# One packed copy in a decoder-layer kernel, issued one tile later behind an order edge

## The chip, the cores and the metric

The kernel runs on one core of a Trainium2 chip. The metric is the device time of one execution in microseconds (us). Three executions before the change took 2226.68, 2227.14 and 2234.79 us, so the median is 2227.14 us. One more execution was taken with the hardware profiler.

## The reference

The reference is one decoder layer on x of 4096 rows by 1024, in float32:

```python
h = _rms(x, norm_gain[l]); proj = h @ w_in[l]          # 1024 -> 3328 columns
y_g = _chunked_gmlp(g_u, g_v, ...) * silu(g_gate)       # 4 heads x 64, chunks of 128 rows
q = _rms(a_q, attn_q_gain); k = _rms(a_k, attn_k_gain)  # 8 heads x 64
y_a = _dilated_attention(q, k, v) * silu(a_gate)        # (window, dilation) = (128,1), (512,4), (2048,16)
y_m = _memory_attention(m_q, mem, ...) * silu(m_gate)   # 4 heads, 256 memory tokens
x = x + concat(y_g, y_a, y_m) @ w_out[l]
```

Queries and keys are normalised for each head (root mean square over 64 values), and the dilated attention reads them in three strides: every row, every 4th and every 16th.

## The kernel before

The 4096 rows are cut into 32 tiles of 128 rows (`NT`). Every large projection is done with 16-bit operands, a value being split into a high and a low part, so that one tile against 512 columns is 24 matmuls (`proj`, L219 to L223).

The work is traced in stages. Pass A (L384 to L459) goes over the 32 tiles: it normalises and transposes three tiles ahead (`rows`), projects the values (`pv`, stored to `vd`), and projects queries and keys of heads 0 to 3 (`pq`). Pass B (`pass_b`) does the queries and keys of heads 4 to 7 (`pqb`) and the attention gates (`pag`). Pass C does the two other branches, and a last loop the output projection (`fps`). The attention proper (`attn_all`) is a generator whose steps are traced between those of pass B and pass C (`merge`) with a higher priority. In it `attn_max` (L465) finds row maxima, and `attn_main` (L533) computes scores, exponentials (`e`, L580), their high part (`ph`, L529) and low part (`pl`, L530) and the products with the values.

The change touches `qk_out` (L292), which both passes call once for each tile, 64 times in all. For a tile n:

- `head_rs` copies the projection out of PSUM on ScalarE (`rw_q`, L257), squares it (L259), sums on VectorE (L261), and takes a power on GpSimd (L269); VectorE multiplies (L276, L278).
- ScalarE casts the result to 16 bit (`hl`, L296), VectorE subtracts for the low part (L297).
- SyncE issues a DMA transpose of `hl` into one half of `stg` (L299). A `stg` tile holds a pair of tiles; there are two of them.
- ScalarE copies this half of `stg` into `stp` with its columns in another order (L300). This is the packed copy. There is one `stp`.
- After the second tile of a pair SyncE issues three stores: `knd` and `qnd` from `stg` (L304, L305) and `qkpd` from `stp` (L306).

In pass A each eighth tile also issues `load_max` for head 0 (L317), which loads back what eight tiles have stored. `attn_max` and `attn_main` of later heads load from the same DRAM tensors.

Each engine runs its instructions in one order, and all DMAs are issued from SyncE's queue, also in one order. That order is not the traced one: a scheduler goes over the whole program with a simulated timeline and takes, for each engine, what is ready by its own times, by priority; the priority is the place in the trace, moved ahead by 400 for the attention steps. Dependences between tiles are found by the framework. An order edge without synchronisation (`tc.issue_after(ins)`) tells the scheduler that what is traced in its block on the engine of `ins` stands behind `ins`.

Of the kernel before, what the change touches and what calls it, by code (L numbers as in the profile page):

```python
# [18 lines left out]
P = 128  # L19
T = 4096  # L20
D = 1024
NT = T // P
# [18 lines left out]
R16 = 16  # L41
# [30 lines left out]
def tile_hybrid_layer(ctx, tc, x, mem, norm_gain, w_in, gv_gain, wsT, gb, aqg, akg,  # L72
                      mem_gain, w_kv, mqg, mkg, w_out, out):
    nc = tc.nc
    V, S, G, TE, Q = nc.vector, nc.scalar, nc.gpsimd, nc.tensor, nc.sync
# [6 lines left out]
    def ps_tile(tag, shape, dt, name):  # L82
        return pp.tile(shape, dt, tag="po" if tag == "tr" else tag, name=name)
# [3 lines left out]
    kn_d = [dp.tile([4, P, T], F16, name=f"knd{g}") for g in range(2)]  # L87
    qn_d = [dp.tile([4, 64, T], F16, name=f"qnd{g}") for g in range(2)]
    qkp_d = [dp.tile([8, P, T], F16, name=f"qkpd{g}") for g in range(2)]
# [109 lines left out]
    def start_job(key, tag, cols, gain, gaina, src=None, pt="pj", pool=None, gap=0):  # L199
        box = []  # L200

        def mk():
            if not box:
                box.append(wtile(tag, 256 * len(cols), key))
            return box[0]

        jobs.append(prep_job(key, [(mk, 256 * i, w_in if src is None else src, c, gain, gaina)
                                   for i, c in enumerate(cols)], pt, pool, gap))
        next(jobs[-1])

    def tick():
        for j in list(jobs):
            if next(j, 1) == 1:
                jobs.remove(j)

    def got(key):
        return ready[key][0][0], [sc for _, sc in ready[key]]

    def proj(ps, xt, w, n, c=0):  # L219
        for k in range(KT):  # L220
            for a, b in ((0, 0), (0, 1), (1, 0)):
                TE.matmul(ps[:, :n], xt[:, a, k, :], w[:, b, k, c:c + n],  # L222
                          start=(k == 0 and a == 0 and b == 0), stop=(k == KT - 1 and a == 1))  # L223
# [50 lines left out]
    def qk_split(pool, ps, nh, scs, nm, gain=None, glo=0):  # L274
        r, qn = head_rs(pool, ps, nh, scs, [S24] * len(scs), nm)
        V.tensor_tensor(qn, qn, bcast(r, HD), ALU.mult)  # L276
        if gain is not None:
            V.tensor_mul(qn[:, glo:nh, :], qn[:, glo:nh, :], gain)  # L278
        return qn
# [9 lines left out]
    sk = ctx.enter_context(tc.tile_pool(name="sk", bufs=2))  # L289
    pm = ctx.enter_context(tc.tile_pool(name="pm", bufs=2))  # L290

    def qk_out(pool, ps, n, g, scs, stgs):  # L292
        stg, stp = stgs
        qn = qk_split(pool, ps, 8, scs, f"q{g}_{n}", agn, 4)
        hl = pool.tile([P, 8, 2, HD], F16, name=f"hl{g}_{n}", tag="hl", bufs=2)
        S.copy(hl[:, :, 0, :], qn)  # L296
        V.tensor_sub(hl[:, :, 1, :], qn, hl[:, :, 0, :])  # L297
        half = slice((n % 2) * P, (n % 2 + 1) * P)
        Q.dma_start_transpose(stg[:, :, half], hl.rearrange("p s a c -> p (s a c)"))  # L299
        S.copy(stp[:, :, half].rearrange("p s (r j) -> p s r j", r=R16),  # L300
               stg[:, :, half].rearrange("p s (j r) -> p s r j", r=R16))
        if n % 2 == 1:
            cc = slice((n - 1) * P, (n + 1) * P)
            Q.dma_start(kn_d[g][:, :, cc].rearrange("s p t -> p s t"), stg[:, 4:8, :])  # L304
            Q.dma_start(qn_d[g][:, :, cc].rearrange("s p t -> p s t"), stg[0:64, 0:4, :])  # L305
            Q.dma_start(qkp_d[g][:, :, cc].rearrange("s p t -> p s t"), stp)  # L306

    def stages(n):
        return (pm.tile([P, 8, 256], F16, name=f"stg{n}", tag="stg", bufs=2),
                pm.tile([P, 8, 256], F16, name=f"stp{n}", tag="stp", bufs=1))  # L310
# [6 lines left out]
    def load_max(h, c0, c1):  # L317
        g, s = h // 4, h % 4
        if h not in heads:
            heads[h] = (sk.tile([P, T], F16, name=f"qn_{h}", tag="qn", bufs=1),  # L320
                        sk.tile([P, T], F16, name=f"kp_{h}", tag="kp", bufs=1))
        qn, kp = heads[h]
        Q.dma_start(kp[:, c0:c1], qkp_d[g][4 + s, :, c0:c1])
        Q.dma_start(qn[0:64, c0:c1], qn_d[g][s, :, c0:c1])
        Q.dma_start(qn[64:128, c0:c1], qn_d[g][s, :, c0:c1])
# [11 lines left out]
    with tc.tile_pool(name="pA", bufs=2) as pA:  # L337
# [44 lines left out]
        stg = None  # L382
        mTs = sk.tile([P, 2, 2, KT, P], F16, name="mTs", tag="q1", bufs=1)
        for n in range(NT):  # L384
# [45 lines left out]
            if n % 2 == 0:  # L430
                stg = stages(f"A{n}")
            qk_out(pm, ps, n, 0, scQ0, stg)
            if n % 8 == 7:
                load_max(0, (n - 7) * P, (n + 1) * P)
            tick()
            if n == 5:
# [4 lines left out]
            if n == 12:  # L441
                wM, scM = got("wM")
                for j in range(2):
# [5 lines left out]
                    hl = pm.tile([P, 8, 2, HD], F16, name=f"mhl{j}", tag="hl", bufs=2)  # L449
# [228 lines left out]
    def pass_b():  # L678
        xTs = {}
        wQ1, scQ1 = got("wQ1")  # L680
        stg = None
        for n in range(NT + LAG):
            if n < NT:
                xT = sk.tile([P, 2, KT, P], F16, name=f"xTb{n}", tag="xT", bufs=4)
                Q.dma_start(xT.rearrange("p a k t -> p (a k t)"), xT_d[n])
                xTs[n] = xT
                ps = ps_tile("pj", [P, 512], F32, f"pqb{n}")
                proj(ps, xT, wQ1, 512)
                if n % 2 == 0:
                    stg = stages(f"B{n}")  # L690
                qk_out(pm, ps, n, 1, scQ1, stg)
                yield
            tick()
            if n == 2:
                wAG, scAG = got("wAG")
                for i in range(2):
                    V.tensor_scalar_mul(hsc[:, i:i + 1], scAG[i][:, 2:3], 0.5)
                    V.tensor_mul(fag[:, i:i + 1], hsc[:, i:i + 1], scV[i][:, 0:1])
                    V.tensor_scalar_mul(fag[:, i:i + 1], fag[:, i:i + 1], 2.0 ** -4)
            if n >= LAG:  # L700
                m = n - LAG
                ps = ps_tile("pj", [P, 512], F32, f"pag{m}")
                proj(ps, xTs.pop(m), wAG, 512)
                sg = pm.tile([P, 512], F32, name=f"sg{m}", tag="sg", bufs=2)
                for i in range(2):
                    S.activation(sg[:, i * 256:(i + 1) * 256], ps[:, i * 256:(i + 1) * 256],
                                 AF.Tanh, scale=hsc[:, i:i + 1])
                V.scalar_tensor_tensor(sg, sg, 1.0, ps, ALU.add, ALU.mult)
                Q.dma_start(ag_d[m], sg)
                yield  # L710
            if n == 6:
                start_job("wC1", "w1", (C_GV, C_MQ), ng, nga)
            if n == 16:
                start_job("wC3", "wc", (C_MG,), ng, nga)
            if n == NT - 1 + CS:
                start_job("wC2", "w2", (C_GU, C_GG), ng, nga, gap=1)

    merge(tc, pass_b(), side, 190/62.0, 2)

    yTs = {}  # L720
# [270 lines left out]
```

## Time and profile before

| | |
|---|---|
| median of three executions | 2227.14 us |
| profiled execution | 2231.72 us, of which its span is 2230.0 us |
| mean granted TensorE clock | 0.966 of full speed |
| TensorE matmul busy | 2031.2 us (91%) |
| VectorE busy | 1459.8 us (65%) |
| ScalarE busy | 1200.2 us (54%) |
| GpSimd busy | 684.2 us (31%) |
| DMA traffic | 341 MB, mean 153 GB/s |

The profiled execution lies 4.6 us above the median and between the fastest and the slowest of the three. In the trace, PE is TensorE's matmul part, PEld its weight load, DVE VectorE, ACT ScalarE, POOL GpSimd and SP SyncE; "q" behind an engine's name is its sequencer. L300 is line 300 of the kernel. Busy matmul time is modelled at its ends, so idle PE time is the surer reading.

### The profile page before, as it was taken

To read this page: it belongs to the slowest core of one execution; us is meant where nothing else is said; L and a number is where in the kernel's file an instruction comes from. 1 tells how busy PE (TensorE), PEld (TensorE's weight loads), DVE (VectorE), ACT (ScalarE), POOL (GpSimd) and SP (SyncE) were. 2 spreads that over 40 slices of the span, in tenths; PEclk is the share of its full clock that TensorE was granted. 3 is DMA by queue.
4 is the path that set the end of the run, shared out by engine and by line. 5 is a ranking of instruction groups with operands and counts; after the bars stand their busy time and mean duration, and the time that the engine had idled before them with its cause. 6 is when DMAs were issued, how large, how long until landed. Compare 5 with 4: busy or idle time off the path is not lost. (4 is left out here: it accounts for less than half of the span.)

```text
span 2230.0 us, 45732 instructions
## 1 busy us (share of the span) xinstructions
PE 2031.2 (91%) x17025; PEld 1297.4 (58%) x17025; DVE 1459.8 (65%) x4331; ACT 1200.2 (54%) x2048; POOL 684.2 (31%) x632
## 2 busy tenths in 40 slices
PE   5989989889889898899999898998997999999999
PEld 4435444334346455465676675775764766666676
DVE  7555564365657676477786677875876667777662
ACT  6666565343457577476565565664655763222221
POOL 1212212121035355253454453553543551000000
PEclk8999999999899999999999999999998999999999
DMA  7767676484565865755646447536435337777662
GB/s 228 198 152 207 167 187 163 115 212 121 153 145 136 205 147 130 202 119 146 167 98 138 116 94 169 114 94 151 97 90 124 89 97 219 222 218 220 205 187 75
DMA packets 468959, 341.00 MB, mean 153 GB/s; under 512 B 294400, under 2 KB 404096, under 8 KB 466944
## 3 DMA queue, kind: packets, MB, share of 16 engines
q1 hardware_dynamic: 468736, 338.08, 58.8%
q8 instruction: 133, 2.18, 0.4%
q14 instruction: 90, 0.74, 0.1%
HBM read 198.52 MB, written 113.84 MB: 140 GB/s over the span
## 5 line engine op out<-in xcount | busy, mean ns | idle before, releaser
L530 POOL TENSOR_TENSOR pl<-e,ph 128x512 f16<-128x512 f32 (+1 forms) x384 | 413.1, 1088 | 359.2 <-ACT ph L529 265.2
L222 PE MATMUL pc<-wC,xTc 128*128 128x512 f16 (+1 forms) x2304 | 473.3, 349 | 6.3 <-DVE zm L899 5.2
L483 DVE CUSTOM_DVE_ANT_0 jk<-pa,mask 128x256 bf16<-128x256 f32 (+1 forms) x768 | 299.8, 390 | 86.1 <-PE pa L476 66.2
L222 PE MATMUL fps<-wO,fyT 128*128 128x256 f16 (+1 forms) x2304 | 341.0, 309 | 0.3 <-DVE fa L746 0.3
L222 PEld LDWEIGHTS <-xTc 128*128 128x128 f16 x2304 | 221.5, 100 | 161.6 <-issue 16.8
L580 ACT ACTIVATE e<-e,gas 128x512 f32<-128x512 f32 (+1 forms) x384 | 254.0, 674 | 112.5 <-DVE e L578 110.5
L578 DVE TENSOR_TENSOR e<-s,mask 128x512 f32<-128x512 f32 (+1 forms) x384 | 234.1, 626 | 77.8 <-PE s L575 68.3
L222 PEld LDWEIGHTS <-fyT 128*128 128x128 f16 x2304 | 224.5, 98 | 103.3 <-issue 1.7
L222 PEld LDWEIGHTS <-xTa 128*128 128x128 f16 x1608 | 159.4, 100 | 205.8 <-issue 42.3
L222 PEld LDWEIGHTS <-xTb 128*128 128x128 f16 x1536 | 150.8, 100 | 174.3 <-issue 29.1
L269 POOL TENSOR_TENSOR r_q<-r_q,mhalf 128x8 f32<-128x8 f32 x64 | 113.2, 1769 | 422.5 <-DVE r_q L267 406.9
L529 ACT CAST ph<-e 128x512 f16<-128x512 f32 (+1 forms) x384 | 211.9, 568 | 18.0 <-PE o L600 11.7
L222 PE MATMUL pqb<-wQ,xTb 128*128 128x512 f16 x768 | 191.6, 393 | 8.6 <-DMA xTb<-xTd 8.2
L222 PE MATMUL pag<-wAG,xTb 128*128 128x512 f16 x768 | 191.6, 389 | 8.0 <-ACT rw_q L257 4.3
L573 PE MATMUL s<-q,k 128*128 128x256 f16 (+1 forms) x768 | 178.8, 264 | 17.9 <-DVE e L578 7.0
L222 PE MATMUL pv<-wV,xTa 128*128 128x512 f16 (+1 forms) x840 | 180.8, 373 | 13.6 <-DVE vt L285 13.0
L222 PE MATMUL pq<-wQ,xTa 128*128 128x512 f16 x768 | 176.0, 385 | 18.3 <-ACT rw_q L257 15.3
L596 PE MATMUL o<-vr,ph 128*128 128x65 f16 x1368 | 173.0, 194 | 7.2 <-ACT ph L529 7.0
L476 PE MATMUL pa<-kp,qn 128*128 128x256 f16 (+1 forms) x768 | 137.8, 270 | 41.4 <-DVE mx L483 25.3
L575 PE MATMUL s<-q,k 65*128 65x256 f16 (+1 forms) x768 | 171.2, 264 | 1.9 <-DMA q<-cm 1.9
L598 PE MATMUL o<-vr,ph 128*128 128x64 f16 x1368 | 171.0, 194 | 0.0
L600 PE MATMUL o<-vr,pl 128*128 128x65 f16 x1368 | 161.1, 193 | 8.4 <-POOL pl L530 7.8
(282 smaller groups left out, 3356.5 us busy)
## 6 DMA issues: line engine op xcount, KB each, us to landing
vr<-vd SPq DMA_DIRECT2D x48, 520.0 KB
fo<-od SPq DMA_DIRECT2D x96, 260.0 KB
od<-ot SPq DMA_DIRECT2D x128, 130.0 KB
x_a<-in_x_dram SPq DMA_DIRECT2D x32, 512.0 KB
xTd<-xTa SPq DMA_DIRECT2D x32, 512.0 KB
xTb<-xTd SPq DMA_DIRECT2D x32, 512.0 KB
xTc<-xTd SPq DMA_DIRECT2D x32, 512.0 KB
fx<-in_x_dram SPq DMA_DIRECT2D x32, 512.0 KB
```

The source lines that it names most:

```text
L222: TE.matmul(ps[:, :n], xt[:, a, k, :], w[:, b, k, c:c + n], start=(k == 0 and a == 0 and b == 0), stop=(k == KT - 1 and a == 1))
L476: TE.matmul(pa[:, i, 256 - w:256], qn[:, q0:q0 + (P - 1) * d + 1:d], packed(kp, d, r, max(b - 1, 0), w), start=True, stop=True)
L483: V.tensor_tensor_reduce(jk[:, :w], pa[:, i, 256 - w:256], masks[d][:, 256 - w:256], 1.0, -3e38, ALU.add, ALU.max, mx[:, mc:mc + 1])
L529: S.copy(ph[:, :w], e[:, :w])
L530: G.tensor_sub(pl[:, :w], e[:, :w], ph[:, :w])
L573: TE.matmul(st[:, i, :n], k1[:, kk], packed(q1, d, r, b, n), start=True, stop=False)
L575: TE.matmul(st[:, i, :n], k2[:, kk], packed(q2, d, r, b, n), start=False, stop=True)
L578: V.tensor_tensor(e[:, :w], st.rearrange("p a q -> p (a q)")[:, :w], masks[d][:, :w], ALU.add)
L580: S.activation(e[:, :w], e[:, :w], AF.Exp, scale=asg[:, 2:3])
L596: TE.matmul(o[:, slot, 0:65], hi[:, c:c + 128], v[:, 0:65], start=(j == 0), stop=False)
L598: TE.matmul(o[:, slot, 0:64], hi[:, c:c + 128], v[:, 66:130], start=False, stop=False)
L600: TE.matmul(o[:, slot, 0:65], lo[:, c:c + 128], v[:, 0:65], start=False, stop=(j == len(terms) - 1))
```

## The change

The packed copy and the three stores become a function `pack` that is put on a list. The list is emptied in the next tile's `qk_out`, behind its cast and its subtraction and ahead of its DMA transpose, inside `tc.issue_after(cast.ins)`: on ScalarE the copy of tile n stands behind the cast of tile n+1. The stores are on SyncE and get no edge. Two more places empty the list, without an edge: in pass A before each `load_max` (tiles 7, 15, 23 and 31), and in pass B after the last tile. No instruction is added or dropped, and no buffer changes in number or size.

```diff
+    late = []
+    def flush():
+        while late:
+            late.pop(0)()
...
-        S.copy(hl[:, :, 0, :], qn)
+        cast = S.copy(hl[:, :, 0, :], qn)
         V.tensor_sub(hl[:, :, 1, :], qn, hl[:, :, 0, :])
+        with tc.issue_after(cast.ins):
+            flush()
         half = slice((n % 2) * P, (n % 2 + 1) * P)
         Q.dma_start_transpose(stg[:, :, half], hl.rearrange("p s a c -> p (s a c)"))
-        S.copy(stp[:, :, half]..., stg[:, :, half]...)
-        if n % 2 == 1:
-            ... three Q.dma_start
+        def pack(n=n, g=g, stg=stg, stp=stp, half=half):
+            S.copy(stp[:, :, half]..., stg[:, :, half]...)
+            if n % 2 == 1:
+                ... the same three Q.dma_start
+        late.append(pack)
...
             qk_out(pm, ps, n, 0, scQ0, stg)
             if n % 8 == 7:
+                flush()
                 load_max(0, (n - 7) * P, (n + 1) * P)
...
                 qk_out(pm, ps, n, 1, scQ1, stg)
                 yield
+            if n == NT - 1:
+                flush()
```

## Rows read from the trace of the kernel before

**Rows 1.** Busy time by stretch: us, then each engine's busy us, PE clock, DMA.
```profile
80.00:458.00 378.00, 344.40 (x1868) 167.24 (x1867) 187.19 (x433) 218.48 (x300) 72.22 (x82) 0.97 0.66 168
486.00:1006.00 520.00, 465.07 (x3614) 268.91 (x3613) 335.50 (x1135) 308.19 (x532) 184.48 (x156) 0.95 0.62 154
1006.00:1846.00 840.00, 770.83 (x8176) 553.33 (x8174) 609.57 (x1921) 508.36 (x999) 401.44 (x353) 0.97 0.50 120
1846.00:2230.00 384.00, 375.10 (x2919) 261.81 (x2916) 248.69 (x607) 100.99 (x102) 2.87 (x3) 0.99 0.65 192
```
**Rows 2.** Line 300, its copies and what ScalarE idled for before them (us, times).
```profile
L300 ACT COPY stpA<-stgA x32: 2020/2042/2060, 80.8 to 479.7; 128x1024 f16<-128x1024 f16 x32
L300 ACT COPY stpB<-stgB x32: 2029/2052/2117, 486.7 to 1003.1; 128x1024 f16<-128x1024 f16 x32
  DMA stgA<-hl: 104.6, 29
  DMA stgB<-hl: 98.8, 28
```
**Rows 3.** Timeline of a pass A tile: start, us, engine, line, what [idle before, releaser].
```profile
403.40 0.62 ACT L296 CAST hl<-rw_q 128x512 f16<-128x512 f32 x1 [3.63 <-DVE rw_q L278]
404.77 1.30 SPq L299 DMA_TRANSPOSE stgA<-hl  x1
408.42 2.03 ACT L300 COPY stpA<-stgA 128x1024 f16<-128x1024 f16 x1 [4.40 <-DMA stgA<-hl]
410.36 0.58 ACT L257 COPY rw_q<-pq 128x512 f32<-128x512 f32 x1
410.99 5.34 PE L222 MATMUL pq<-wQ,xTa 128*128 128x512 f16 x24 [1.62 <-ACT rw_q L257]
416.49 0.62 ACT L296 CAST hl<-rw_q 128x512 f16<-128x512 f32 x1 [3.63 <-DVE rw_q L278]
```
**Rows 4.** Timeline of TensorE, one pass A tile without idle time.
```profile
85.13 1.06 PE L248 MATMUL pta<-idh,xh_a 128*128 128x128 f16 x16
96.43 1.06 PE L248 MATMUL pta<-idh,xh_a 128*128 128x128 f16 x16
```
**Rows 5.** Waits in 85 to 486 us: us in total, times, longest.
```profile
PE pq L222 <- ACT rw_q L257: 15.3, 10, 2.4
PE pv L222 <- DVE vt L285: 13.0, 3, 8.9
```
**Rows 6.** Timeline around tile 16 of pass A.
```profile
280.36 2.25 SPq L299 DMA_TRANSPOSE stgA<-hl  x1
286.83 2.02 ACT L300 COPY stpA<-stgA 128x1024 f16<-128x1024 f16 x1 [9.83 <-DMA stgA<-hl]
295.59 6.90 PE L222 MATMUL pv<-wV,xTa 128*128 128x512 f16 x24 [8.94 <-DVE vt L285]
```
**Rows 7.** Timeline of TensorE, three further pq of pass A.
```profile
373.45 5.34 PE L222 MATMUL pq<-wQ,xTa 128*128 128x512 f16 x24 [0.63 <-ACT rw_q L257]
424.62 7.03 PE L222 MATMUL pq<-wQ,xTa 128*128 128x512 f16 x24 [1.85 <-ACT rw_q L257]
451.17 7.03 PE L222 MATMUL pq<-wQ,xTa 128*128 128x512 f16 x24 [2.43 <-ACT rw_q L257]
```
**Rows 8.** Waits in 486 to 1006 us, the same columns.
```profile
DVE r_q L261 <- ACT sq_q L259: 52.0, 23, 4.8
PE pa L476 <- DVE mx L483: 13.0, 13, 3.3
PE pqb L222 <- DMA xTb<-xTd: 8.2, 5, 3.2
PE o L596 <- ACT ph L529: 7.0, 10, 1.2
PE pag L222 <- ACT rw_q L257: 4.3, 2, 2.7
```
**Rows 9.** SyncE's own waits in 486 to 1006 us.
```profile
SPq L306 <- ACT stpB L300: 9.1, 11, 0.9
```

More of the change, by code (lines that the diff above doesn't have):

```diff
@@ L295, in qk_out @@
         hl = pool.tile([P, 8, 2, HD], F16, name=f"hl{g}_{n}", tag="hl", bufs=2)
-        S.copy(hl[:, :, 0, :], qn)
+        cast = S.copy(hl[:, :, 0, :], qn)
         V.tensor_sub(hl[:, :, 1, :], qn, hl[:, :, 0, :])
+        with tc.issue_after(cast.ins):
+            flush()
         half = slice((n % 2) * P, (n % 2 + 1) * P)
         Q.dma_start_transpose(stg[:, :, half], hl.rearrange("p s a c -> p (s a c)"))
-        S.copy(stp[:, :, half].rearrange("p s (r j) -> p s r j", r=R16),
-               stg[:, :, half].rearrange("p s (j r) -> p s r j", r=R16))
-        if n % 2 == 1:
[L303 to L306, printed above, removed]
+        def pack(n=n, g=g, stg=stg, stp=stp, half=half):
+            S.copy(stp[:, :, half].rearrange("p s (r j) -> p s r j", r=R16),
+                   stg[:, :, half].rearrange("p s (j r) -> p s r j", r=R16))
+            if n % 2 == 1:
+                cc = slice((n - 1) * P, (n + 1) * P)
+                Q.dma_start(kn_d[g][:, :, cc].rearrange("s p t -> p s t"), stg[:, 4:8, :])
+                Q.dma_start(qn_d[g][:, :, cc].rearrange("s p t -> p s t"), stg[0:64, 0:4, :])
+                Q.dma_start(qkp_d[g][:, :, cc].rearrange("s p t -> p s t"), stp)
+        late.append(pack)
     def stages(n):
```

## The prediction

> **What bounds the kernel now.** I read the busy time by stretch first, then the waits of each stretch, then single tiles in the timeline. The stretches [rows 1] show that TensorE sets the pace everywhere: it is busy 344.40 of 378 us in pass A's steady part, 465.07 of 520 in pass B, 770.83 of 840 in the middle of the attention, 375.10 of 384 at the end. Its idle time is what a change can take away: 33.6 us in pass A and 54.9 us in pass B. The 78 us behind 1006 lie after the last packed copy [rows 2], so I expect nothing from there.
>
> The line of the packed copy [rows 2] shows 64 copies of 2.04 and 2.05 us, ahead of which ScalarE idled 104.6 and 98.8 us for the DMA transpose that feeds them. ScalarE runs one queue, so everything behind the copy waited too. One tile shows who [rows 3]: cast at 403.40, transpose issued at 404.77, copy from 408.42 (4.40 us of idle ScalarE), and only then the copy of the next projection out of PSUM at 410.36. TensorE, which needs that PSUM buffer, had stood still for 1.62 us when it began at 410.99. The next cast comes at 416.49, so this loop takes 13.09 us a tile. TensorE's own work on a tile takes 96.43 - 85.13 = 11.30 us where nothing delays it [rows 4]. In such tiles the loop over cast, transpose, packed copy and PSUM copy is what is late, not TensorE.
>
> **The change, part by part.**
>
> Removed: the wait of the copy for its own transpose. Tile n's copy now stands behind the cast of tile n+1. The transpose lands 408.42 - 404.77 = 3.65 us after its issue [rows 3], and the next cast is some 11 us later, so in the steady part it has landed. The loop is then: PSUM copy to next cast 416.49 - 410.36 = 6.13 us, cast 0.62, packed copy 2.03, together 8.78 us [rows 3]. That is below 11.30 [rows 4], and TensorE is late next, with 2.5 us to spare.
>
> Pass A, price: TensorE's waits for that PSUM copy are 15.3 us in 10 places [rows 5]. One of them, 0.63 us, is at tile 23 [rows 7], where the list is emptied at once and nothing changes; 14.7 remain. The largest single gap, 8.94 us ahead of a pv, is named after VectorE but starts from the packed copy of tile 16, which held ScalarE for 9.83 us until 286.83 [rows 6]; its transpose had been issued beside reloads and took 6.5 us. Behind the cast of tile 17 it would be waited for by nobody. The matmuls that follow idle time run slower: 24 of them take 6.90, 7.03 and 7.03 us [rows 6, 7] against 5.34 [rows 3], 4.9 us together. The sum for pass A is 14.7 + 8.9 + 4.9 = 28.5 us.
>
> Not all of it comes back. In nine tiles plus tile 16 another wait will take part of the place; the nearest row is the 0.63 us that is left at tile 23 [rows 7], so 10 x 0.63 = 6 us off. I take 22 us. The bounds are 0, if other waits fill every gap, and 33.6, all idle time of the stretch [rows 1].
>
> Pass B, price: the waits that have ScalarE's queue as their cause are 4.3 us (pag for the PSUM copy) and 7.0 us (attention products for `ph`) [rows 8]. The copy itself stays in the queue with its 2.05 us, so of the 7.0 I take a half; with 4.3 that is 8, less what new waits take: 5 us. Upper bound: VectorE, too, stands 52.0 us behind ScalarE's squares, and TensorE waits 13.0 us for VectorE's maxima [rows 8]; if these went as well, 4.3 + 7.0 + 13.0 = 24 us. Lower bound: -51 us, by the slower case below.
>
> Moved on ScalarE: 64 x 2.04 = 131 us of copies, none more or less. They are hidden as shown, by the 2.5 us of slack a tile. At tiles 7, 15, 23 and 31 two copies fall into one tile (tile n-1's behind the cast, tile n's at once, with its wait as before): at most 4 x 2.03 = 8 us if nothing hides them; I take nothing, since tile 23 lost only 0.63 with its wait in full [rows 7].
>
> Moved on SyncE: 96 stores (32 tile pairs, three each), one tile later. They pass the loads, the value stores and the next transposes in that queue. `stp` is single: tile n+2's copy must wait until the `qkpd` store has been read out, but copy and store move together, so the distance stays one tile. `stg` is double and loses one of its tiles of distance; two remain. If the scheduler puts the transpose of tile n+1 behind the `qkpd` store, it waits for the packed copy, 2.03 us after the cast instead of the subtraction; this is 1.4 us of a transpose that nobody waits for until the next cast.
>
> The order edges are no instructions: nothing.
>
> **A rule on DMA completion.** After reloads in the same queue the transpose landed later: 286.83 - 280.36 = 6.5 us [rows 6] against 3.65 [rows 3]. The Trainium skill, "DMA: Bandwidth & Descriptors", section "Queues, rings and completion order", says that a DMA's semaphore step lands only after every earlier write of that DMA engine, whatever the queue. The rows agree in direction. The rule speaks against the change, since the three stores of a pair are now issued right ahead of a transpose instead of a tile before it; by it the sum would be that of the first rival.
>
> **The sum.** 22 + 5 = 27 us. From the profiled execution, 2231.7 us, this gives 2204.7; that execution lies 4.6 us above the median of the three, from which the same sum gives 2200.1. I predict 2202 us, midway (2229 less 27; the rivals below start from 2229 too). Its own range, with 18 to 37 us gained, is 2192 to 2212.
>
> **The rivals.**
>
> *Transposes land late behind the stores.* In each pair the even tile's transpose follows three stores, and takes 6.5 us [rows 6] or longer. For: that row. Against: cast to transpose takes 1.4 us, some 4 with the stores ahead, and 4 + 6.5 is still within the 11.30 of a tile; the loop has 2.5 us in hand besides. If it costs 1 us in each of the 12 pairs of pass A whose stores are put off, the gain falls to 15 us: 2214 us.
>
> *VectorE and the attention are set free as well.* With 200 us less waiting on ScalarE [rows 2], the maxima in pass B no longer stand behind squares. For: the 52.0 us [rows 8]. Against: TensorE had other work in nearly all of that time. Pass A 28 and pass B 24: 52 us, about 2177 us.
>
> *SyncE is blocked (slower).* The `qkpd` store waits for a copy that now waits for the next tile's cast, and all loads behind it in SyncE's one queue stand still. In pass B TensorE already lost 3.2 us where a load of `xTb` came late [rows 8]. If each of 16 pairs does that, 51 us are lost against 27 gained: +24, 2253 us. It decides from about 9 pairs on. Against: SyncE's waits on the packed copy are 9.1 us in 11 places, never above 0.9 [rows 9], and the scheduler places the store where its own timeline has the copy done.
>
> *The order changes without effect.* The scheduler orders the whole program anew; gaps in the stretch behind 1006, 69 us up to 1846 [rows 1], may shift either way and eat the gain. 2229 us, give or take 8.
>
> **How the numbers follow.** Forecast 0.50; late transposes 0.20; more set free 0.12; no effect 0.09; SyncE blocked 0.09. A change below 0.5%, 11 us, is about what a measurement here can't tell from none, so faster means below 2216. Forecast and more set free lie there, and somewhat more than half of late transposes: 0.50 + 0.12 + 0.11 = 0.73. Same: the rest of that, and most of no effect, 0.09 + 0.07 = 0.16. Slower: SyncE blocked and the rest, 0.11. The range for 8 in 10 leaves out the far end of "more set free" and most of the slower case: 2174 to 2231.
>
> **What would show it.** Right: ScalarE's idle time ahead of line 300 falls from 203 us to below 50, what is left being at tiles 7, 15, 23, 31 and a few uneven ones; the tiles from 390 to 450 take 11.3 to 11.8 us instead of 13.1; the gap ahead of 295.59 is gone; the stretch of pass A is some 20 us shorter; the rest keeps its length within 10 us. Wrong: the wait ahead of line 300 stays long (late transposes), SyncE's wait for line 306 grows to several us and TensorE's waits for `xTb` with it (blocked), or pass A shrinks and a stage behind 1006 grows as much (no effect).

## The result: 3.6% faster, three times the predicted gain

The changed kernel takes 2150.93 us (median of four executions, 2147.33 to 2154.39) against 2230.43 us for the kernel before (four, 2226.68 to 2234.79). The ratio is 0.9643, 95% interval 0.9612 to 0.9673. The forecast was 2202 us with a range down to 2174: the direction was right, and so was the cause in passes A and B; the size was not. 79.5 us are gone where 27 had been summed.

The stages show where. I cut both traces at the first `pqb` (start of pass B), the first `pc` (start of pass C) and the first `fps` (last loop). These are the two rows of the kernel before that the groups ahead of the prediction do not hold, pass B and pass C in full; columns as in [rows 1].

```profile
458.00:1016.10 558.10, 496.42 (x3798) 284.78 (x3797) 366.04 (x1244) 331.07 (x576) 197.23 (x164) 0.95 0.63 158
1016.10:1853.40 837.30, 768.13 (x8143) 551.38 (x8142) 607.58 (x1908) 501.68 (x979) 397.26 (x349) 0.97 0.50 120
```

And the changed kernel: pass A, pass B, pass C and the last loop.

```profile
80.00:423.50 343.50, 336.62 (x1875) 165.51 (x1874) 188.50 (x439) 218.87 (x299) 74.85 (x82) 1.00 0.75 184
423.50:948.50 525.00, 483.38 (x3815) 284.25 (x3814) 364.74 (x1245) 332.48 (x584) 197.06 (x165) 0.97 0.69 171
948.50:1770.00 821.50, 772.06 (x8128) 553.23 (x8126) 605.98 (x1901) 499.75 (x976) 394.14 (x348) 0.97 0.50 121
1770.00:2146.40 376.40, 367.35 (x2859) 257.31 (x2856) 241.90 (x593) 98.50 (x99) 2.33 (x2) 0.99 0.65 191
```

| stage | before, us | after, us | change | of it TensorE idle | of it TensorE busy |
|---|---|---|---|---|---|
| pass A from 80 us | 378.0 | 343.5 | -34.5 | 33.6 to 6.9 | 344.4 to 336.6 |
| pass B | 558.1 | 525.0 | -33.1 | 61.7 to 41.6 | 496.4 to 483.4 |
| pass C | 837.3 | 821.5 | -15.8 | 69.2 to 49.4 | 768.1 to 772.1 |
| last loop | 376.6 | 376.4 | -0.2 | | |

The sum is 83.6 us, the difference of the two spans (2230.0 and 2146.4). The busy column matters too. The number of matmuls hardly differs (pass B even has 17 more of the attention's), but the granted clock rose from 0.97 to 1.00 in pass A and from 0.95 to 0.97 in pass B, so 7.8 and 13.0 us of the gain are shorter matmuls, not removed gaps.

The mechanism is read from the packed copy's line, which answers to [rows 2] (line 300 is now line 310):

```profile
L310 ACT COPY stpA<-stgA x32: 2028/2047/2062, 83.1 to 444.8; 128x1024 f16<-128x1024 f16 x32
L310 ACT COPY stpB<-stgB x32: 2028/2065/2143, 453.8 to 932.3; 128x1024 f16<-128x1024 f16 x32
  DMA stgA<-hl: 13.1, 4
  DMA stgB<-hl: 6.2, 2
```

The same 64 copies of the same length, and ScalarE idles 19.3 us ahead of them instead of 203.4. One tile of pass A in the timeline, ScalarE first, answers to [rows 3]:

```profile
367.00 0.62 ACT L302 CAST hl<-rw_q 128x512 f16<-128x512 f32 x1 [1.96 <-DVE rw_q L278]
367.52 2.04 ACT L310 COPY stpA<-stgA 128x1024 f16<-128x1024 f16 x1
369.62 0.58 ACT L257 COPY rw_q<-pq 128x512 f32<-128x512 f32 x1
```

The copy stands right behind the cast, with no idle time, and the next copy out of PSUM follows 2.6 us after the cast began (6.96 us in [rows 3]). TensorE in the same stretch shows no gap:

```profile
358.17 1.06 PE L248 MATMUL pta<-idh,xh_a 128*128 128x128 f16 x16
359.06 5.34 PE L222 MATMUL pv<-wV,xTa 128*128 128x512 f16 x24
364.24 5.34 PE L222 MATMUL pq<-wQ,xTa 128*128 128x512 f16 x24
369.42 1.06 PE L248 MATMUL pta<-idh,xh_a 128*128 128x128 f16 x16
```

A tile takes 369.42 - 358.17 = 11.25 us, the tile of [rows 4], where the loop took 13.09. TensorE's waits in pass A (80 to 423.5 us) answer to [rows 5]:

```profile
PE pv L222 <- DVE vt L285: 5.2, 3, 3.5
PE pa L489 <- DMA kp<-qkpd: 1.5, 1, 1.5
PE ptm L248 <- ACT mTs L250: 0.2, 1, 0.2
```

The wait of `pq` for ScalarE's copy, 15.3 us before, is not there any more. In pass B (423.5 to 948.5 us) the waits that answer to [rows 8] are these, the first VectorE's, the rest TensorE's:

```profile
DVE r_q L261 <- ACT sq_q L259: 32.0, 21, 3.4
```

```profile
PE pa L489 <- DVE mx L496: 10.9, 9, 3.7
PE pa L489 <- DMA qn<-qnd: 10.6, 2, 7.4
PE o L609 <- ACT ph L542: 3.4, 5, 1.1
PE o L613 <- POOL pl L543: 3.1, 7, 0.6
PE pag L222 <- ACT rw_q L257: 2.1, 2, 2.0
```

The wait of `pqb` for the load of `xTb` (8.2 us) has no row left. GpSimd's `pl` was in no row of [rows 8]; over the whole of pass B (458 to 1016.1 us) the maxima and `pl` had cost this before:

```profile
PE pa L476 <- DVE mx L483: 15.4, 16, 3.3
PE o L600 <- POOL pl L530: 5.9, 14, 0.8
```

SyncE's wait for the packed copy in pass B, which [rows 9] give as 9.1 us in 11 places, fell too:

```profile
SPq L316 <- ACT stpB L310: 4.5, 4, 1.8
```

### The profile page after: what moved, and what is told of

Its sections match the earlier page's. It is cut to its first block, busy times and chain, and to the rows that moved or that the text cites. A ratio compares the mean times of both kernels' runs of the same rounds, so it can differ in the third digit from the quotient of the medians.

```text
span 2146.4 us, 45733 instructions
## 1 busy us (share of the span) xinstructions
PE 2015.0 (94%) x17025; PEld 1297.6 (60%) x17025; DVE 1457.5 (68%) x4331; ACT 1199.4 (56%) x2048; POOL 682.5 (32%) x632
## 4 chain that ended last, share of the span: by engine, by line
PE 40%; DMA 9%; DVE 7%; ACT 3%; issue 2%; SPq 1%; POOL 1%; ACTq 0%; DVEq 0%; POOLq 0%
PE fps L222 14%; PE pc L222 11%; PE s L586 2%; PE s L588 2%; PE pa L489 2%; DMA od<-ot 1%; DMA qm<-q2t 1%; DVE e L591 1%; DMA cm<-rw 1%; PE fpt L771 1%; DVE jk L496 1%; PE pqb L222 1%; PE pag L222 1%; DMA fo<-od 1%; PE o L613 1%
## 5 line engine op out<-in xcount | busy, mean ns | idle before, releaser
L222 PEld LDWEIGHTS <-xTc 128*128 128x128 f16 x2304 | 222.9, 100 | 161.0 <-issue 11.8
L542 ACT CAST ph<-e 128x512 f16<-128x512 f32 (+1 forms) x384 | 211.0, 568 | 26.7 <-PE o L613 19.9
L222 PE MATMUL pag<-wAG,xTb 128*128 128x512 f16 x768 | 186.1, 383 | 2.2 <-ACT rw_q L257 2.1
```

What stands on the lines that cost most here:

```text
L222: TE.matmul(ps[:, :n], xt[:, a, k, :], w[:, b, k, c:c + n], start=(k == 0 and a == 0 and b == 0), stop=(k == KT - 1 and a == 1))
L542: S.copy(ph[:, :w], e[:, :w])
```

## The experiments

My theory: ScalarE's wait for the transpose, in its one queue, held up everything in passes A and B, and the rest of the gain is pass C under another order of the program. Rivals: the reordering alone brings pass B too; the trace place without the edge does it; the late stores matter; the late place of the copy matters and not the wait.

Stage lengths in the table are of the profiled execution. The runs were made on different chips, whose kernel before took 2233.48, 2250.15, 2251.18 and 2248.66 us; a ratio is always against the same chip.

| kernel | us | ratio, 95% | pass A | pass B | pass C |
|---|---|---|---|---|---|
| a_only | 2171.79 | 0.974 (0.9711 to 0.9769) | 340.2 | 558.2 | 816.8 |
| b_only | 2188.11 | 0.9807 (0.977 to 0.9843) | 380.3 | 534.2 | 814.7 |
| no_edge | 2231.75 | 0.9994 (0.9973 to 1.0015) | 377.6 | 553.1 | 834.8 |
| dbl_before | 2271.06 | 1.0088 (1.0063 to 1.0113) | 396.3 | 584.0 | 828.0 |
| dbl_after | 2177.77 | 0.9677 (0.9646 to 0.9708) | 349.1 | 561.8 | 809.2 |
| c_prio400 | 2232.36 | 0.9914 (0.9884 to 0.9944) | 388.4 | 566.5 | 823.4 |
| c_prio100 | 2244.66, one execution | | 382.3 | 563.3 | 841.6 |
| stores_now | 2158.92 | 0.9591 (0.9558 to 0.9623) | 347.6 | 529.6 | 828.7 |
| two_late | 2179.33 | 0.9678 (0.9659 to 0.9697) | 346.6 | 532.1 | 839.8 |
| load_late | 2176.52 | 0.9657 (0.9627 to 0.9687) | 341.7 | 540.2 | 820.3 |
| pack_dve | 2181.25 | 0.9697 (0.9663 to 0.9731) | 338.8 | 534.3 | 846.6 |
| wait_back | 2230.94 | 0.9921 (0.9901 to 0.9941) | 375.2 | 542.3 | 850.3 |

Two things limit what the stage columns can tell. One profiled execution stands behind each: kernels whose engines have the same order in a pass (before, no_edge, c_prio400, c_prio100, and b_only in pass A) took 377.6 to 388.4 us in pass A and 553.1 to 566.5 us in pass B. And the stages do not hold the same work: a new order also moves attention steps over the border between pass B and pass C. Of the 4104 matmuls of the attention's products (`o`), 1262 (two_late) to 1443 (load_late) stand in pass B, 1350 before and 1359 after the change.

**Only pass A late (a_only), only pass B late (b_only).** The changed kernel, with the list emptied at once in the other pass.

```diff
         late.append(pack)
+        if g == 1:        # a_only; b_only has g == 0
+            flush()
```

> Only pass A's packed copies are put off; pass B's are issued at once. Theory 1 (ScalarE is set free in the stage whose copies move): pass A up to the first pqb matmul takes 423 to 427 us as with the whole change, pass B up to the first pc matmul 550 to 562 us as before, whole time about 2230 - 34 = 2196, within 10. Theory 2 (the new order of the whole program is better, wherever the copies stand): pass B shortens too, to 540 or less, and the whole time is below 2185. Pass C, which has no packed copy, decides a third point: by theory 1 its 837 (before) and 822 us (after) are two draws of one order or another, and it lies anywhere from 815 to 845 here.

> Only pass B's packed copies are put off. Theory 1: pass A takes 458 us as before, pass B 520 to 532 us (33 us less than before), whole time about 2197, within 15, and the gains of a_only and b_only add up to the 64 to 68 us that passes A and B gained together. Theory 2: the gains don't add; pass B stays above 540 since pass A's order is the old one.

Pass B of a_only and pass A of b_only, the passes that were left as before:

```profile
420.20:978.40 558.20, 496.30 (x3838) 287.18 (x3837) 369.72 (x1258) 335.41 (x586) 200.95 (x166) 0.95 0.63 160
```

```profile
80.00:460.30 380.30, 345.73 (x1897) 168.40 (x1895) 187.91 (x437) 221.91 (x304) 73.42 (x83) 0.97 0.68 168
```

Both have the length and the clock of the kernel before (558.1 and 378.0 us, 0.95 and 0.97). In pass A of b_only the engines' order is still that of the kernel before; in pass B of a_only it is another one, and it gained nothing. Each pass became shorter only where its own copies were late: 37.8 us in A, 23.9 us in B, together 61.7 us, a little less than the 64 to 68 I had expected. The time of a_only is below what I had expected, and even below the 2185 us that I had named for theory 2, though its pass B did not shorten: pass C is 20.5 us shorter (22.6 us in b_only), and no packed copy runs there.

**The trace place without the edge (no_edge).**

```diff
-        with tc.issue_after(cast.ins):
-            flush()
+        flush()
```

> The whole change without the order edge: the list is emptied at the same place of the trace, only issue_after is left out. ScalarE's, VectorE's, GpSimd's and TensorE's orders are then those of the kernel before. Theory 1: ScalarE waits 200 us for the transposes as before and the time is 2230 within 6 us. A rival by which the later trace place or the later stores give the gain: below 2200.

ScalarE's idle time ahead of the copy, pass A's copies and pass B's, is back at 198.1 us:

```profile
  DMA stgA<-hl: 104.1, 27
  DMA stgB<-hl: 94.0, 26
```

With the trace changed and the edge left out, ScalarE, VectorE, GpSimd and TensorE have exactly the order of the kernel before, SyncE all but a stretch of it: the scheduler puts the copy back to where its own timeline has the transpose done. The edge is the change.

**The wait alone put back (wait_back).** The changed kernel; behind each transpose ScalarE copies one column of it into a scratch tile that nothing reads.

```diff
         Q.dma_start_transpose(stg[:, :, half], hl.rearrange(...))
+        tch = pool.tile([P, 1], F16, name=f"tch{g}_{n}", tag="tch", bufs=2)
+        S.copy(tch, stg[:, 0, (n % 2) * P:(n % 2) * P + 1])
```

> The changed kernel with the wait alone put back: behind each transpose ScalarE copies one column (128x1) of its result into a scratch tile that nothing reads, so it waits there for the tile's own transpose, as it did before, while the packed copy and its stores stay one tile late. ScalarE stands in most tiles with this tiny copy ahead of the next copy of a projection out of PSUM. My theory (the wait of ScalarE's in-order queue is what cost the time in both passes, the named waits on loads, on GpSimd and on the clock included): ScalarE's idle time ahead of the tiny copy is 180 to 240 us, pass A is 370 to 390 us long (343.5 in the changed kernel), pass B 545 to 575 us (525.0), and the run comes to 2195 to 2240 us, depending on what pass C (809 to 847 over orders) does. Rival one (pass B gained through another order of the engines, or through the late place of the copy, not through the wait): pass A 370 to 390 us, pass B 520 to 535 us. Rival two (the late place is what counts in both): 340 to 350 and 520 to 535 us, 2150 to 2175 us in all.

The packed copies stay late and wait for nothing. The tiny copies take 0.19 us each and wait 144.6 us, less than the 180 to 240 I had expected:

```profile
  DMA stgB<-hl: 72.7, 26
  DMA stgA<-hl: 71.9, 23
```

Pass A and pass B (columns as above):

```profile
80.00:455.20 375.20, 350.28 (x1907) 170.04 (x1906) 189.27 (x440) 224.12 (x335) 75.47 (x83) 0.97 0.71 171
455.20:997.50 542.30, 490.05 (x3697) 281.67 (x3696) 365.29 (x1226) 330.65 (x602) 190.70 (x159) 0.96 0.66 163
```

Pass A grows by 31.7 us, nearly all that the change had taken. But for the tiny copies the engines have nearly the changed kernel's order there, so in pass A the wait is nearly the whole cause, clock and all (TensorE's busy time rises from 336.6 to 350.3). Pass B grows by 17.3 of its 33.1 us, between my theory's 545 and the rival's 535. (This run's chip is 0.8% slower than that of the changed kernel's profile, which is 3 us of pass A and 4 of pass B.)

But pass B has another order in this run, and less of the attention stands in it. TensorE's matmuls of scores (`s`) and products (`o`) in pass B, the changed kernel's and then this run's (stretch, its length, busy us, times, clock, DMA):

```profile
423.50:948.50 525.00, 74.01 (x536) 0.97 0.69 171
455.20:997.50 542.30, 70.38 (x504) 0.96 0.66 163
423.50:948.50 525.00, 66.57 (x1359) 0.97 0.69 171
455.20:997.50 542.30, 64.03 (x1283) 0.96 0.66 163
```

32 scores and 76 products have moved to pass C. At the changed kernel's 0.138 and 0.049 us each, they are some 8 us of TensorE (an estimate). With them pass B would take some 550 us, which is inside my theory's range, and some 25 us of the gain would be back, 21 without the slower chip's part. Of the 17.3 us, 10.6 are idle time, and they have names, which the waits of TensorE in pass B give:

```profile
PE o L611 <- ACT ph L544: 10.0, 9, 1.9
PE o L615 <- POOL pl L545: 7.0, 12, 1.1
```

These two together are 17.0 us, against 3.4 + 3.1 = 6.5 in the changed kernel. Over the kernels they mostly follow ScalarE's wait in pass B: 11.9 to 13.6 us together in before, no_edge and a_only, 5.4 to 6.8 in after, b_only, stores_now, load_late and pack_dve, but 11.1 in two_late. The wait for `xTb` does not come back, but it follows neither the wait nor the place: it is 1.3 us in a_only, whose copies of pass B are early, and 3.9 us in b_only, whose copies are late. So by this estimate 21 to 25 of the 33.1 us of pass B's gain are the wait, though only 72.7 of its 98.8 us were put back. What the rest hangs on, the late place of the copy, the order or the spread between executions, this run does not tell.

**The transpose doubled (dbl_before, dbl_after).** A second transpose of `hl` into a scratch tile stands ahead of the true one, in the kernel before and in the changed one, so that the true one lands later.

```diff
+        scr = pool.tile([P, 8, P], F16, name=f"scr{g}_{n}", tag="scr", bufs=1)
+        Q.dma_start_transpose(scr, hl.rearrange("p s a c -> p (s a c)"))
         Q.dma_start_transpose(stg[:, :, half], hl.rearrange("p s a c -> p (s a c)"))
```

> The kernel before, with each DMA transpose of a query-key tile preceded by a second one of the same source into a scratch tile that nobody reads, so that the true one lands later. By theory 1 (ScalarE's wait for the transpose is in the loop that sets the pace): it lands 1.3 to 3.5 us later, ScalarE's idle time ahead of the packed copy grows from 203 us to 280 to 400, pass A grows from 378 to 405 to 450 us, pass B from 558 to 575 to 620. By a rival, in which the wait itself was hidden and the change gained by another order on SyncE's queue: both stages grow by less than 10 us.

> The changed kernel with the same scratch transposes. By theory 1 the later landing is covered by the tile in between: ScalarE's idle time ahead of the packed copy stays below 50 us, pass A at 343 to 352, pass B at 525 to 545. By the rival it grows as much as the kernel before does.

A miss. The wait that I meant to lengthen hardly moved in the kernel before (ScalarE's waits, 80 to 1000 us):

```profile
ACT stpA L302 <- DMA stgA<-hl: 111.7, 29, 11.7
ACT stpB L302 <- DMA stgB<-hl: 98.2, 26, 8.9
```

That is 209.9 us against 203.4. The extra transposes loaded SyncE and the DMA engines instead (in pass B the DMA engines' busy share rose from 0.63 to 0.71 and from 0.69 to 0.76), and pass B grew in both kernels (to 584.0 and 561.8). The pair tells nothing apart for pass B. In pass A the changed kernel took them with 5.6 us more (349.1), on a chip 0.9% slower, where the kernel before took 18.3 us more; this fits a transpose for which nobody waits.

**The stores left in their old place (stores_now).** `knd` and `qnd` are issued right behind their own transpose; only the copy and `qkpd` are late.

> The changed kernel, but the two stores from stg (knd, qnd) are issued in their old place; only the packed copy and its own store come a tile later, behind the edge. ScalarE's, VectorE's, GpSimd's and TensorE's orders are those of the changed kernel. Theory 1: the moved copy is all that counts, 2150 us within 8 (ratio to before 0.961 to 0.968). Rival by which the later stores give part of the gain: 2165 or more.

The order of the engines is that of the changed kernel, but for a stretch on SyncE. The ratio, 0.9591, is a little below the range I had expected, and its interval overlaps that of the change (0.9643). But the edit moved next to nothing: in the changed kernel too the scheduler kept `knd` and `qnd` right behind their transposes. So this run repeats the change, and what these two stores would give or cost a tile later is not shown.

**One tile later still (two_late), `load_max` one tile later (load_late), the copy on VectorE (pack_dve).** Three attempts to get more:

```diff
-            flush()
+            flush(1)                      # two_late: one copy stays on the list
```

```diff
-            if n % 8 == 7:
+            if n % 8 == 0 and n:          # load_late, and once more at the end
+                load_max(0, (n - 8) * P, n * P)
```

```diff
-        with tc.issue_after(cast.ins):    # pack_dve: behind the subtraction
+        with tc.issue_after(low.ins):
...
-            S.copy(stp...)
+            V.tensor_copy(stp...)
```

> The packed copy and its stores two tiles later instead of one. Theory 1: one tile already covers the landing of the transpose in all but a few tiles (ScalarE's idle time ahead of the copy is 19 us in 6 places), so passes A and B gain at most 5 us more: 2140 to 2160. Rival (late transposes still cost in pass B): 2130 or less.

> The changed kernel, with load_max of pass A one tile later too, so that tiles 7, 15 and 23 no longer empty the list at once. By theory 1 three of the four waits left in pass A go (13 us of ScalarE), which TensorE hardly feels: pass A 338 to 344 instead of 343.5, whole time 2140 to 2152. Rival: the later reloads hold up the attention's maxima, and the time grows.

> The changed kernel with the packed copy on VectorE, behind the next tile's subtraction, instead of on ScalarE. ScalarE loses 131 us of work in passes A and B, VectorE gets 64 copies of 0.7 to 1.1 us. If ScalarE's work itself (not its wait) still holds TensorE, pass B shrinks by 5 to 15 us: 2135 to 2145; if VectorE's maxima are what is late next in pass B, it grows: 2155 to 2175. I hold the second for likelier.

All three keep the gain in pass A (338.8 to 346.6 us) and most of it in pass B (532.1 to 540.2), and none is faster than the change. stores_now, which has the changed kernel's order, ran on the same chip with a ratio of 0.9591; all three stay above its interval. Where they lose against it, the stage columns alone would tell wrongly, for the attention moves; at the costs above (estimates again):

- two_late's pass C, 11.1 us longer, holds 97 products and 40 scores more, some 10 us that its pass B lacks. So its loss stands in pass B, at the same work some 13 us longer; the copies, in both passes, wait 15.7 us for the one `stp` to be stored.
- load_late's pass B, 10.6 us longer, holds 84 products and 16 scores more, some 6 us. Its profiled execution, 2165.6 us, lies 11 us below its median, so most of its loss is not in the trace.
- pack_dve's pass C, 17.9 us longer, holds some 7 us more of the attention, and pass B, 4.7 us longer, lacks them. In its pass B TensorE's wait for VectorE's maxima is 27.8 us, against 10.9 in the changed kernel; this is the outcome that I had held for likelier:

```profile
PE pa L489 <- DVE mx L496: 27.8, 16, 6.7
```

**Pass C by itself (c_prio400, c_prio100).** In the kernel before the largest wait of pass C is one place, where TensorE waits 15 us for a transpose of the memory branch (`qm`): its source was ready at 1675 us, and SyncE issued it only behind a train of the attention's loads and stores. The waits of TensorE in pass C, the place itself in TensorE's timeline, and the issue in SyncE's:

```profile
PE ms L804 <- DMA qm<-q2t: 24.0, 5, 15.0
```

```profile
1694.69 0.26 PE L804 MATMUL ms<-qm,K2m 65*128 65x128 f16 x1 [15.01 <-DMA qm<-q2t]
```

```profile
1690.54 1.27 SPq L793 DMA_TRANSPOSE qm<-q2t  x1
```

The experiment moves this transpose ahead in the scheduler's priorities, in the kernel before.

```diff
-        Q.dma_start_transpose(Q2m, q2t.rearrange("p s c -> p (s c)"))
+        with tc.high_priority(offset=400):     # c_prio100: 100
+            Q.dma_start_transpose(Q2m, q2t.rearrange("p s c -> p (s c)"))
```

> The kernel before, its packed copies untouched; only in pass C the second DMA transpose of the memory queries (L793, from q2t) is given a priority higher by 400. All engines' orders are those of before up to pass B's end, and other ones behind it. Theory 1c (the 16 us that pass C gained are those of an order that happens to lack one 15 us wait for that transpose): passes A and B 378 and 558 us as before, pass C 810 to 825, whole time 2208 to 2220. Rival: pass C's gain came from what passes A and B do earlier (loads done earlier, clock); then pass C stays at 830 to 840.

> The same with a priority higher by 100, one look: another draw of pass C's order, passes A and B as before. Theory 1c: pass C 810 to 830 unless this order has a long wait of its own.

With 400 the wait shrinks from 24.0 to 7.2 us and pass C to 823.4 us, while passes A and B, whose order is unchanged, are 10.4 and 8.4 us longer than in the profile of before (the chip of that run is 0.9% slower, which is some 3 and 5 us of it):

```profile
PE ms L805 <- DMA qm<-q2t: 7.2, 4, 2.7
```

```profile
1034.90:1858.30 823.40, 773.02 (x8144) 553.11 (x8143) 609.72 (x1900) 502.85 (x979) 395.20 (x349) 0.97 0.52 121
```

The ratio is 0.9914, some 18 us (2250.15 to 2232.36) from one edit that has nothing to do with the packed copy. With 100 the same wait goes as well (6.2 us), but others of 8.1 us (`zm`) and 6.4 us (`q`) take its place and pass C stays at 841.6, outside the range I expected; I had allowed for a long wait of its own. In the changed kernel the wait for `qm` is small without any such edit, by TensorE's waits from 948.5 to 1770 us:

```profile
PE ms L819 <- DMA qm<-q2t: 2.2, 3, 1.0
```

Its order in pass C is another one, and that transpose happens to be issued in time.

## Why the prediction was right or wrong

**Which loop is late: right.** The wait ahead of the copy fell to 19.3 us (below 50 had been the sign), the tile to 11.25 us (11.3 to 11.8), and the wait of `pq` for ScalarE is gone. a_only, no_edge and wait_back confirm it for pass A from three sides: late copies 340.2, wait back 375.2, no edge 377.6 us.

**Pass A, 22 us: the sum stood too low by 12.5.** The step that failed is "in nine tiles plus tile 16 another wait will take part of the place", the deduction of 6 us. Hardly any wait took the place: the waits of `pv` other than the one of 8.94 us were 4.1 us before and are 5.2, and even the 0.63 us of tile 23 went. Idle time fell by 26.7 us where 14.7 + 8.9 - 6 = 17.6 had been summed. The rest is the clock: I counted three groups of slow matmuls, 4.9 us, and busy time fell by 7.8 us.

**Pass B, 5 us: the term that was mis-sized most, 33.1 measured.** Two steps failed. The first is "the waits that have ScalarE's queue as their cause are 4.3 us ... and 7.0 us": I took as caused by ScalarE only those waits that bear its name, and half of one of them. These two rows fell about as priced (4.3 to 2.1 and 7.0 to 3.4, 5.8 us together), but all idle time fell by 20.1 us, with GpSimd's `pl` (which waits for `ph`), `xTb` and the maxima in it. The other step is that there was no clock term for pass B at all; busy time fell by 13.0 us, from 0.95 to 0.97 of the clock. wait_back shows that most of this is the wait: it brings back 17.3 us as measured (10.5 in the rows of `ph` and `pl`, 6.7 in busy time), and 21 to 25 by the estimate with the attention that moved. What of the remaining 8 to 12 us is the copy's place, the order or the spread between executions, these runs do not tell apart; that order alone did nothing is shown only for an order with early copies (a_only, 558.2).

**Behind 1006 us, "I expect nothing from there": wrong by 16 us.** The step looked only for what the change touches. The order edge made the scheduler place the whole program anew: between 82 us (VectorE) and 142 us (GpSimd) each of the five engines leaves the order of the kernel before, and pass C has another order too. Over the fourteen kernels here pass C took between 809 and 850 us; some 13 us of that are attention that the order puts into pass B or pass C (dbl_after against wait_back, at the costs above), the rest is other waits and the spread between executions. The kernel before had a poor order there, with a 15 us wait that one priority could mend, and the changed kernel's was better. That this one wait is the whole of the 16 us is not shown, since c_prio100 is without it and no shorter. This part of the gain is luck of the order, and another edit may lose it again, as pack_dve did in part. It is also why "no effect", with its give or take 8, was the wrong size for the scheduler's part.

**What was costed at nothing.** The 131 us of copies stayed hidden, as forecast. The double copies at tiles 7, 15, 23 and 31 cost at most their own waits, 11.2 us of ScalarE at the last three of them (the other 1.9 of the 13.1 us are at tile 0), of which TensorE shows nothing in pass A. The 96 stores: the scheduler issued only `qkpd` later, so the price of the others is not shown.

**The rivals.** Late transposes: no, 19.3 us of waits are left. By the Trainium skill, "DMA: Bandwidth & Descriptors", section "Queues, rings and completion order", a DMA is counted as done only after the earlier writes of its DMA engine, which would make a transpose behind stores late; this trace gives the rule little occasion, since `knd` and `qnd` are issued where they were, 2.5 us or more ahead of the next transpose, and `qkpd` stands behind that transpose in 20 of 32 pairs. SyncE blocked: no, its wait for the copy halved in pass B and TensorE's wait for `xTb` is gone. "VectorE and the attention are set free as well", 2177 us, was nearest in size, at 0.12, but not by its own mechanism: VectorE's wait behind the squares fell only from 52.0 to 32.0 us, and TensorE's for the maxima from 15.4 to 10.9. It too lacked the clock and pass C.

## What to carry to other kernels

When a wait in an in-order queue goes, do not price it only by the waits that bear that engine's name. Take all the idle time of the stage as the bound, and give the clock a term of its own: here a late ScalarE showed up as late GpSimd and as matmuls at a lower clock. Under this list scheduler the place in the trace decided nothing and the order edge decided; and the edge was a new draw for every stage behind it. So read the stages that an edit doesn't touch before crediting the edit with the total, look there for a single long wait that a priority can mend, and count the work in a stage before comparing its length over orders.

## What was not expected of the hardware

The same reordering copy of 128x1024 16-bit values takes VectorE little more than half of ScalarE's 2.04 us, as its line in pack_dve shows:

```profile
L310 DVE COPY stpA<-stgA x32: 1079/1087/1102, 83.3 to 441.0; 128x1024 f16<-128x1024 f16 x32
```

It brought no more than the change did: ScalarE's 2 us were hidden by then, and TensorE waited longer for VectorE's maxima. And the chips differ: the kernel before took 2230 us beside the changed kernel and 2233 us beside a_only, b_only and no_edge, and 2249 to 2251 us on the three chips of the other runs, 0.7 to 0.9% more, which is more than several of the effects above. So whole times are compared as ratios on one chip, and stage lengths from different chips only for larger differences.
